# Decay selector and low-rank gate of a two-block hybrid layer: products of 48 and 16 contraction rows become products of 128 rows

## The chip, the cores and the metric

The kernel runs on one core of one Trainium2 chip. The metric is the device time of one execution in microseconds; lower is better. Three runs of the kernel before gave 1198.25, 1198.42 and 1198.77 us (median 1198.42). TensorE (PE in the rows) does the matrix products, VectorE (DVE) and ScalarE (ACT) the elementwise work, GpSimd (POOL) a few fills, and SyncE (SP) issues nearly all DMA transfers. PEld is TensorE's weight load, a separate instruction ahead of each product.

## The reference

Two model blocks run one after the other on 256 tokens of width 1024. The change lies in the first block's mixer, which has a state-space half (SSD) and a gated linear attention half (GLA). What matters of it:

```
proj = n @ w_in
z, xBC, dt_raw, q, k, v, r, a1, g_ssd, g_gla = split(proj)
# SSD: 16 heads, decay of each head
dt = softplus(dt_raw + dt_bias);  a = dt * -exp(A_log)
a_cs = cumsum(a)
Lmat = exp(a_cs[l] - a_cs[s]) where l >= s, else 0      # one matrix per head
y_diag = einsum(CB, Lmat, X)
# GLA: the gate comes from a low-rank product, 16 wide
log_alpha = log_sigmoid(a1 @ w_a2 + b_a) / 16            # a1: 256x16, w_a2: 16x512
```

`dt_raw` and `a1` are 16 columns each of `proj`; `w_a2` is a 16x512 matrix.

## The kernel before, in words

All work is laid out by a program that writes each engine's instructions in a fixed order; nothing is reordered at run time. The main stream is a series of `linear` and `tok_half` calls: products of 128x128 weight blocks with activations of 256 columns (272 in the second block), or of 128-token blocks with 512 weight columns. Both operands are split into a high and a low part in the round format fp32r, and three products (high-high, high-low, low-high; lines L403 to L405, or L454 to L456) replace one fp32 product. Such an fp32r product goes through TensorE in one pass, and a plain fp32 product is two MATMUL instructions in the trace, one behind the other.

The weights come in chunks of 8 blocks (512 KB). SP issues the load of each into one of three raw buffers (L136), ACT writes the high part (`whi`, L151), DVE subtracts to get the low part (`wlo`, L162), and so a raw buffer comes free when DVE is done with it.

Everything else is written as generators in `Side`: one step of some of them is put into the stream after every fourth weight block (`beat`, `side.tick`). PE takes what these steps issue in the middle of its stream. The products of the side work use four PSUM banks `psa` in turn (`psum_a`, so the fifth request gets the first bank again), those of the main stream four banks `psm`.

The parts that the change and the prediction speak of:

- `ev_1`, L683: the output of the block `dta1` (dt in rows 0 to 15 and 32 to 47, a1 in rows 64 to 79) is scaled into `da`, which lies in the tile `sr`, as does `wa`, the 16x512 gate matrix, loaded at L698 into rows 64 to 79. L699 and L700 load the constants and the selector.
- `rstd_0`, run in the middle of the first `linear`: the reciprocal norm, L380 and L381 on ACT, three DVE steps, then L683. PE needs L683 before it can go on, since its next output takes that bank.
- `prepare`, L574 to L577: the selector `i2` (48 rows: two unit matrices for the high and the low part of the decays), the mask `neg` and the identity are rounded to fp32r by ACT.
- `gates_gen`, L634 to L638: the running sums of the decays go to `st` (tile name `cst`), rows 0 to 15 high part, rows 32 to 47 low part.
- `decay_gen`, L646: four products for the gate, in fp32 with 16 contraction rows; ACT takes each result with L647 and L648.
- `ssd_cb`, L712 to L716: the products of B and C, a quarter into the stream of `tok_half`, which need the first `Silu` of L667 on ACT.
- `ssd_head`, L728 and L729: for j = 0, 2, 4, 6 two times two transposes (listed under L466), each pair of them into a bank of its own, and DVE scales the result into `xt`.
- `ssd_pair`, run eight times, two heads each: for each head L747 spreads that head's running sums over 128 partitions by the selector (48 contraction rows, 384 columns), L748 adds the mask to 256 of the columns; ACT takes the exponentials (L757), DVE multiplies by `cb` (L762), PE multiplies with `xt` (L768 to L772, 64 output rows for each head), DVE adds up (L776).

The two places of the change's products in the code:

```python
mm(ps, lhsT=wa[64:80, hh * P : (hh + 1) * P], rhs=da[64:80, :], start=True, stop=True)
mm(ps[:, :384], lhsT=i2[:, hd : hd + 1].to_broadcast([48, P]), rhs=st, start=True, stop=False)
```

Of the kernel before, what the change touches and what calls it, by code (L numbers as in the profile page):

```python
# [7 lines left out]
F32 = mybir.dt.float32  # L8
F32R = mybir.dt.float32r
AF = mybir.ActivationFunctionType  # L10
ALU = mybir.AluOpType
# [3 lines left out]
P = 128  # L15
D = 1024
KD = D // P
S = 256
META = 16
T = S + META  # L20
# [5 lines left out]
OFF = {}  # L26
# [204 lines left out]
def body(ctx, tc, w, lruw, vecs, cons, sels, xT, metaT, memT, wa2, gfin, out, dbg=None):  # L231
    nc = tc.nc
    act = nc.scalar.activation
    copy = nc.scalar.copy
    tt = nc.vector.tensor_tensor
    ts = nc.vector.tensor_scalar
    stt = nc.vector.scalar_tensor_tensor
    mm = nc.tensor.matmul
    side = Side()

    cp = ctx.enter_context(tc.tile_pool(name="const", bufs=1))
# [28 lines left out]
    ident = C("ident")  # L270
    eps = cp.tile([P, 1], F32, name="eps")
    nc.vector.memset(eps, EPS)
    one = cp.tile([P, 1], F32, name="one")
    nc.vector.memset(one, 1.0)
    onesD = cp.tile([P, P], F32, name="onesD")
# [17 lines left out]
    def flat(ap):  # L293
        return ap.rearrange("p a b -> p (a b)")
# [191 lines left out]
    def block1():  # L486
# [9 lines left out]
        rst = {}  # L496
# [32 lines left out]
        vG = p.tile([P, 2, D], F32, name="vG")  # L529
        sr = p.tile([P, KD, S], F32, name="sr")  # L530
        macc = p.tile([P, 2, S], F32, name="macc")
        da = sr[:80, 2, :]
        wa = flat(sr)[:80, :512]

        def ev_q(i, ps):
            e = tmp("eq")[:, :S]
# [22 lines left out]
        ssd, ssd_y = ExitStack(), ExitStack()  # L559
        sp = ssd_y.enter_context(tc.tile_pool(name="ssdy", bufs=1))  # L560
        sz = sp.tile([P, KD, S], F32, name="sz")
        st = sp.tile([48, 384], F32R, name="cst")
        i2 = sp.tile([48, 16], F32R, name="i2")
        colT = sp.tile([P, 80], F32, name="colT")
        a48 = sp.tile([P, 2, 48], F32, name="a48")
        sp = ssd.enter_context(tc.tile_pool(name="ssd", bufs=1))
# [4 lines left out]
        sel = xt.rearrange("p a b c -> p (a b c)")[:, :304]  # L571

        def prepare():
            copy(i2, sel[:48, :16])  # L574
            copy(neg, sel[:, 16:])
            copy(identR, ident)
            ts(hgn, vec[:, VEC["gla_norm"] : VEC["gla_norm"] + 2], 0.5, None, ALU.mult)  # L577
            yield
# [23 lines left out]
        def gates_gen():  # L602
            both_t = [P, 2, 16]
            U = C("trile")
            yield
            yield
            ps = psum_a()
            for t in range(2):
                transpose(ps[:, t * 16 : t * 16 + 16], da[:16, t * P : (t + 1) * P])
            v = spt[:, 7, :]  # L610
            tt(
                v.rearrange("p (t h) -> p t h", t=2), ps[:, :32].rearrange("p (t h) -> p t h", t=2),
                vec[:, VEC["dt_bias"] : VEC["dt_bias"] + 16].unsqueeze(1).to_broadcast(both_t), ALU.add,
            )
            eA = spt[:, 6, :16]
            yield
            yield from softplus_small(colT[:, :32], v, [spt[:, i, :] for i in range(6)])
            act(eA, vec[:, VEC["A_log"] : VEC["A_log"] + 16], AF.Exp)
            tabled.append(1)
            nc.gpsimd.memset(flat(a48), 0.0)  # L620
            for c in (0, 32):
                stt(
                    a48[:, :, c : c + 16], colT[:, :32].rearrange("p (t h) -> p t h", t=2), -1.0,
                    eA.unsqueeze(1).to_broadcast(both_t), ALU.mult, ALU.mult,
                )
            yield from rest(5)
            ps = psum_a()
            mm(ps[:, :32], lhsT=U, rhs=a48[:, :, :16], start=True, stop=True)
            mm(ps[:, 32:48], lhsT=one.to_broadcast([P, P]), rhs=a48[:, 0, :16], start=True, stop=True)
            for t in range(2):  # L630
                mm(ps[:48, 64 + t * P : 64 + (t + 1) * P], lhsT=a48[:, t, :], rhs=U, start=True, stop=True)
            yield
            cs = ps[:48, 64 : 64 + S]
            copy(st[:, :S], cs)  # L634
            ts(colT[:, 32:64], ps[:, :32], -1.0, None, ALU.mult)
            tt(colT[:, 64:80], ps[:, 32:48], colT[:, 32:48], ALU.add)
            tt(st[32:48, :S], cs[32:48], st[32:48, :S].bitcast(F32), ALU.subtract)
            nc.vector.tensor_copy(st[:, S:], st[:, P:S].bitcast(F32))  # L638
            show("colT", colT)

        def decay_gen():
            yield
            yield
            for hh in range(4):
                ps = psum_a()[:, :S]
                mm(ps, lhsT=wa[64:80, hh * P : (hh + 1) * P], rhs=da[64:80, :], start=True, stop=True)  # L646
                act(kt[:, hh, :], ps, AF.Identity, bias=V("gla_b_a", hh))  # L647
                act(b16[:, hh, :], ps, AF.Abs, bias=V("gla_b_a", hh))  # L648
                yield
            act(flat(b16), flat(b16), AF.Exp, scale=-1.0)  # L650
            act(flat(b16), flat(b16), AF.Ln, bias=one)
            tabled.append(1)
            yield
            msk = tmp("gm")[:, :S]
            nc.gpsimd.memset(msk, 1.0)
            nc.gpsimd.memset(msk.rearrange("p (c l) -> p c l", l=64)[:, :, 0:1], 0.0)
            for hh in range(4):
                stt(kt[:, hh, :], kt[:, hh, :], 0.0, b16[:, hh, :], ALU.min, ALU.subtract)
                nc.vector.tensor_tensor_scan(b16[:, hh, :], msk, kt[:, hh, :], 0.0, ALU.mult, ALU.add)
                yield  # L660
# [19 lines left out]
        def ev_1(i, ps):  # L680
            what, j = seq[i]
            if what == "d":
                tt(da, ps[:80], rst[0][:80], ALU.mult)  # L683
            elif what == "c":
                conv(j, ps, i < RAW)
            elif i < RAW:
                tt(sz[:, j, :], ps, rst[0], ALU.mult)
            else:
                copy(sz[:, j, :], ps)
# [5 lines left out]
        cols = [{"d": [("dta1", 0)], "z": zc, "c": xc}[a][b] for a, b in seq]  # L695
        side.add(moments())
        side.width = 1
        nc.sync.dma_start(wa[64:80, :], wa2)  # L698
        nc.sync.dma_start(con, cons)  # L699
        nc.sync.dma_start(sel, sels)  # L700
        linear(x, cols[:RAW], ev_1, S, outer=4, mid=rstd_0, at=(2, 7), spare=3)
# [32 lines left out]
                    )  # L734
                yield

        ys = Split(S)

        def ssd_pair(j):
            g = j // 4  # L740
            cps = []
# [2 lines left out]
            for i in range(2):  # L744
                hd = 2 * j + i
                ps = psum_a()
                mm(ps[:, :384], lhsT=i2[:, hd : hd + 1].to_broadcast([48, P]), rhs=st, start=True, stop=False)  # L747
                mm(ps[:, :S], lhsT=identR, rhs=neg[:, 1 : P + 1].unsqueeze(1).to_broadcast([P, 2, P]), start=False, stop=True)  # L748
                cps.append(ps)
            yield  # L750
# [2 lines left out]
            for i in range(2):  # L753
                hd = 2 * j + i
# [800 lines left out]
def matrices(i):  # L1555
    w_in = i["w_in"][0]
    dta1 = np.zeros((D, P), np.float32)
    dta1[:, :16] = dta1[:, 32:48] = w_in[:, OFF["dt"] : OFF["dt"] + 16]
    dta1[:, 64:80] = w_in[:, OFF["a1"] : OFF["a1"] + 16]
    return {  # L1560
        "w_in": w_in, "dta1": dta1, "w_up_ssd": i["w_up_ssd"][0], "w_up_gla": i["w_up_gla"][0],
        "w_o": i["w_o"][0], "w_xq": i["w_xq"][0], "w_xkv": i["w_xkv"][0], "w_xo": i["w_xo"][0],
        "w_ffn_in": i["w_ffn_in"][0], "w_ffn_out": i["w_ffn_out"][0], "w_qkv": i["sb_w_qkv_2"][0],
        "w_so": i["sb_w_o_2"][0], "w_lin": i["lru_w_in_2"][0], "w_lout": i["lru_w_out_2"][0],
        "mlp_up0": i["mlp_w_up_2"][0], "mlp_dn0": i["mlp_w_down_2"][0],
        "mlp_up1": i["mlp_w_up_2"][1], "mlp_dn1": i["mlp_w_down_2"][1],
    }
# [27 lines left out]
```

## Time and profile before

| | us |
|---|---|
| median of three runs | 1198.42 |
| the profiled execution | 1197.76 |
| its span, first to last instruction | 1195.9 |
| PE busy | 1172.1 |
| DVE busy | 813.0 |
| ACT busy | 692.7 |

The profile is of one execution, and its rows add up to that one's time: 1.86 us lie around the span, and the execution stands 0.66 us below the median of the runs. A product's duration in a row includes its way through the array, which overlaps the next product; what a product costs in a stream is the distance between its start and the next one's start.

### The profile page before, as it was taken

To read this page: it belongs to the slowest core of one execution; us is meant where nothing else is said; L and a number is where in the kernel's file an instruction comes from. 1 tells how busy PE (TensorE), PEld (TensorE's weight loads), DVE (VectorE), ACT (ScalarE), POOL (GpSimd) and SP (SyncE) were. 2 spreads that over 40 slices of the span, in tenths; PEclk is the share of its full clock that TensorE was granted. 3 is DMA by queue.
4 is the path that set the end of the run, shared out by engine and by line. 5 is a ranking of instruction groups with operands and counts; after the bars stand their busy time and mean duration, and the time that the engine had idled before them with its cause. 6 is when DMAs were issued, how large, how long until landed. Compare 5 with 4: busy or idle time off the path is not lost.

```text
span 1195.9 us, 22416 instructions
## 1 busy us (share of the span) xinstructions
PE 1172.1 (98%) x9054; PEld 1121.5 (94%) x9054; DVE 813.0 (68%) x1297; ACT 692.7 (58%) x1108; POOL 2.9 (0%) x31
## 2 busy tenths in 40 slices
PE   7999999999999999999999999999999989999997
PEld 7898899899998999999989989999999989999886
DVE  6887767877776877766676657765545887766443
ACT  6577565754655654546576656665444866665333
POOL 0000000000000000000000000000000000000000
PEclk9999999999999999999999999999999989999999
DMA  7555336375644565555623335655555535555652
GB/s 252 181 171 171 124 113 194 106 236 187 193 135 138 178 191 190 182 189 177 194 88 109 122 109 171 215 176 176 177 175 194 158 110 162 190 181 192 193 192 73
DMA packets 56855, 199.23 MB, mean 167 GB/s; under 512 B 7200, under 2 KB 8992, under 8 KB 56496
## 3 DMA queue, kind: packets, MB, share of 16 engines
q1 hardware_dynamic: 56464, 197.35, 51.9%
q8 instruction: 71, 1.16, 0.4%
q10 hardware_dynamic: 288, 0.46, 0.1%
q14 instruction: 32, 0.26, 0.1%
HBM read 196.73 MB, written 1.05 MB: 165 GB/s over the span
## 4 chain that ended last, share of the span: by engine, by line
PE 91%; DVE 3%; ACT 2%; DMA 1%; issue 1%; SPq 0%; DVEq 0%; ACTq 0%
PE psm L403 24%; PE psm L404 24%; PE psm L405 24%; PE psm L1438 2%; PE psm L1439 2%; PE psm L1440 2%; DMA wraw<-in_w_dram 1%; PE psm L454 1%; PE psm L456 1%; PE psm L455 1%; PE psa L1226 1%; ACT whi L151 1%; PE psa L747 0%; DVE iu L1391 0%; PE psa L1201 0%
## 5 line engine op out<-in xcount | busy, mean ns | idle before, releaser
L403 PE MATMUL psm<-sp_hi,whi 128*128 128x256 f32 (+1 forms) x2296 | 656.1, 286 | 7.0 <-ACT whi L151 4.6
L404 PE MATMUL psm<-sp_lo,whi 128*128 128x256 f32 (+1 forms) x2296 | 651.6, 284 | 0.5 <-DVE sp_lo L321 0.2
L405 PE MATMUL psm<-sp_hi,wlo 128*128 128x256 f32 (+1 forms) x2296 | 650.6, 283 | 0.0
L162 DVE TENSOR_TENSOR wlo<-wraw,whi 128x1024 fp32r<-128x1024 f32 (+1 forms) x339 | 412.2, 1217 | 190.1 <-ACT whi L151 186.4
L151 ACT CAST whi<-wraw 128x1024 fp32r<-128x1024 f32 (+1 forms) x339 | 353.1, 1042 | 317.9 <-PE psm L404 221.7
L403 PEld LDWEIGHTS psm<-sp_hi,whi 128*128 128x128 f32 x2296 | 433.7, 189 | 10.2 <-ACT whi L151 4.6
L404 PEld LDWEIGHTS psm<-sp_lo,whi 128*128 128x128 f32 x2296 | 433.3, 189 | 1.7 <-DVE sp_lo L321 0.9
L405 PEld LDWEIGHTS psm<-sp_hi,wlo 128*128 128x128 f32 x2296 | 433.7, 189 | 0.0
L403 PE MATMUL psm<-sp_hi,wx 128*128 128x272 f32 (+1 forms) x192 | 56.5, 294 | 3.1 <-ACT sp_hi L314 3.1
L404 PE MATMUL psm<-sp_lo,wx 128*128 128x272 f32 (+1 forms) x192 | 56.2, 293 | 0.8 <-DVE sp_lo L319 0.8
L405 PE MATMUL psm<-sp_hi,wx 128*128 128x272 f32 (+1 forms) x192 | 56.0, 291 | 0.0
L1438 PE MATMUL psm<-whi,sp_hi 128*128 128x512 f32 x128 | 50.5, 395 | 0.0
L1439 PE MATMUL psm<-wlo,sp_hi 128*128 128x512 f32 x128 | 50.4, 393 | 0.0
L1440 PE MATMUL psm<-whi,sp_lo 128*128 128x512 f32 x128 | 50.3, 393 | 0.0
L403 PEld LDWEIGHTS psm<-sp_hi,wx 128*128 128x128 f32 x192 | 37.2, 194 | 3.4 <-ACT sp_hi L314 3.3
L1499 DVE SCALAR_TENSOR_TENSOR mr<-psm,rstd 128x272 f32<-128x272 f32 (+1 forms) x64 | 27.3, 431 | 18.6 <-PE psm L405 18.4
L162 DVE TENSOR_TENSOR wx<-wraw,wx 128x1024 fp32r<-128x1024 f32 x24 | 29.4, 1223 | 14.7 <-ACT wx L151 14.7
L151 ACT CAST wx<-wraw 128x1024 fp32r<-128x1024 f32 x24 | 25.1, 1048 | 23.9 <-PE psm L404 20.5
L404 PEld LDWEIGHTS psm<-sp_lo,wx 128*128 128x128 f32 x192 | 37.1, 193 | 1.2 <-DVE sp_lo L319 1.1
L405 PEld LDWEIGHTS psm<-sp_hi,wx 128*128 128x128 f32 x192 | 37.1, 193 | 0.0
L316 ACT ACTIVATE sp_hi<-h,vec 128x256 fp32r<-128x256 f32 (+1 forms) x56 | 28.3, 510 | 6.8 <-DVE h L1408 3.4
L364 DVE TENSOR_TENSOR acc<-acc,sq 128x256 f32<-128x256 f32 (+1 forms) x63 | 26.8, 426 | 5.8 <-ACT sq L359 5.2
(384 smaller groups left out, 1226.5 us busy)
## 6 DMA issues: line engine op xcount, KB each, us to landing
wraw<-in_w_dram SPq DMA_DIRECT2D x366, 512.0 KB, 3.6
kTm<-in_memT_dram SPq DMA_DIRECT2D x1, 1024.0 KB, 5.1
gw<-in_lruw_dram SPq DMA_DIRECT2D x1, 1024.0 KB, 6.0
h<-in_xT_dram SPq DMA_DIRECT2D x3, 256.0 KB, 6.2
out_dram<-yT SPq DMA_DIRECT2D x2, 288.0 KB, 2.2
fin<-in_gfin_dram SPq DMA_DIRECT2D x1, 512.0 KB, 5.0
out_dram<-yT ACTq DMA_DIRECT2D x2, 224.0 KB, 2.6
h<-in_xT_dram SPq DMA_DIRECT2D x2, 128.0 KB, 2.5
```

The costliest lines, as they stand in the source:

```text
L151: self.nc.scalar.copy(hi[:, s], self.raw[self.done][:, s])
L162: self.nc.vector.tensor_tensor(lo[:, s], raw[:, s], hi[:, s].bitcast(F32), ALU.subtract)
L316: act(hi, src, AF.Copy, scale=scale)
L364: tt(self.acc, self.acc, sq, ALU.add)
L403: mm(ps, lhsT=wh, rhs=xh, start=start, stop=False)
L404: mm(ps, lhsT=wh, rhs=xl, start=False, stop=False)
L405: mm(ps, lhsT=wl, rhs=xh, start=False, stop=stop)
L454: mm(ps, lhsT=x.hi[:, k, s], rhs=wh, start=k == 0, stop=False)
L1438: mm(ps, lhsT=hid.hi[:, k, s], rhs=w[0], start=False, stop=False)
L1439: mm(ps, lhsT=hid.hi[:, k, s], rhs=w[1], start=False, stop=False)
L1440: mm(ps, lhsT=hid.lo[:, k, s], rhs=w[0], start=False, stop=k == kk - 1)
L1499: stt(t_, ps, 0.0, rst[0], ALU.max, ALU.mult)
```

## The change

The two kinds of small product get 128 contraction rows. For the selector, `i2` and `st` become 128 rows high; the rows that carried nothing are zero (`st` is filled with zeros by GpSimd, `i2` takes the zero rows of the selector input). For the gate, the three part products (high-high, high-low, low-high) are stacked in the rows of one fp32r product: the weights for `a1` stand three times in `dta1`, so that `da` holds a1 in rows 32, 64 and 96 onward; `wa2` is loaded three times; ACT rounds both, and DVE replaces 16 rows of each by the low part. The new tiles `wa3` and `da3` lie in the buffer `ys`, which is set up earlier for that.

```diff
+    zero = cp.tile([P, 1], F32, name="zero")
+    nc.gpsimd.memset(zero, 0.0)
...
-        da = sr[:80, 2, :]
-        wa = flat(sr)[:80, :512]
+        LOW_W, LOW_A = slice(32, 48), slice(96, 112)
+        da = sr[:, 2, :]
+        wa = flat(sr)[:, :512]
+        ys = Split(S)
+        da3 = ys.hi[:, 0, :]
+        wa3 = ys.room[0][:, 2 * T : 2 * T + 512]
...
-        st = sp.tile([48, 384], F32R, name="cst")
-        i2 = sp.tile([48, 16], F32R, name="i2")
+        st = sp.tile([P, 384], F32R, name="cst")
+        i2 = sp.tile([P, 16], F32R, name="i2")
...
         def prepare():
-            copy(i2, sel[:48, :16])
+            copy(i2, sel[:, :16])
+            nc.gpsimd.tensor_copy(st, zero.to_broadcast([P, 384]))
+            copy(wa3, wa)
+            tt(wa3[LOW_W], wa[LOW_W], wa3[LOW_W].bitcast(F32), ALU.subtract)
+            copy(da3, da)
+            tt(da3[LOW_A], da[LOW_A], da3[LOW_A].bitcast(F32), ALU.subtract)
...
-            copy(st[:, :S], cs)
+            copy(st[:48, :S], cs)
...
-            nc.vector.tensor_copy(st[:, S:], st[:, P:S].bitcast(F32))
+            nc.vector.tensor_copy(st[:48, S:], st[:48, P:S].bitcast(F32))
...
-                mm(ps, lhsT=wa[64:80, hh * P : (hh + 1) * P], rhs=da[64:80, :], start=True, stop=True)
+                mm(ps, lhsT=wa3[:, hh * P : (hh + 1) * P], rhs=da3, start=True, stop=True)
...
-                tt(da, ps[:80], rst[0][:80], ALU.mult)
+                tt(da, ps, rst[0], ALU.mult)
...
-        nc.sync.dma_start(wa[64:80, :], wa2)
+        nc.gpsimd.memset(wa, 0.0)
+        for row in (32, 64, 96):
+            nc.sync.dma_start(wa[row : row + 16, :], wa2)
...
-                mm(ps[:, :384], lhsT=i2[:, hd : hd + 1].to_broadcast([48, P]), rhs=st, start=True, stop=False)
+                mm(ps[:, :384], lhsT=i2[:, hd : hd + 1].to_broadcast([P, P]), rhs=st, start=True, stop=False)
...
-    dta1[:, :16] = dta1[:, 32:48] = w_in[:, OFF["dt"] : OFF["dt"] + 16]
-    dta1[:, 64:80] = w_in[:, OFF["a1"] : OFF["a1"] + 16]
+    dta1[:, :16] = w_in[:, OFF["dt"] : OFF["dt"] + 16]
+    for c in (32, 64, 96):
+        dta1[:, c : c + 16] = w_in[:, OFF["a1"] : OFF["a1"] + 16]
```

The order of the instructions on PE stays as it was. On ACT, at `prepare`, just behind the copies of the first half of v (L461), before:

```order
34 L461 COPY vG<-psm 128x512 x2
35 L151 CAST whi<-wraw 128x1024
36 L574 CAST i_176<-xt 48x16
37 L575 CAST neg<-xt 128x288
38 L576 CAST identR<-con 128x128
39 L590 COPY pad<-psm 128x256
```

and now, with `sr` the tile of `wa` and `da`, and `sp_hi` that of `wa3` and `da3`:

```order
34 L463 COPY vG<-psm 128x512 x2
35 L151 CAST whi<-wraw 128x1024
36 L582 CAST i_180<-xt 128x16
37 L584 CAST sp_hi<-sr 128x512
38 L586 CAST sp_hi<-sr 128x256
39 L588 CAST neg<-xt 128x288
40 L589 CAST identR<-con 128x128
41 L603 COPY pad<-psm 128x256
```

Two casts have come in ahead of the copies that empty PE's outputs. On DVE, at the same place, before:

```order
53 L162 TENSOR_TENSOR wlo<-wraw,whi 128x1024 x3
54 L577 TENSOR_SCALAR hgn<-vec 128x2
55 L162 TENSOR_TENSOR wlo<-wraw,whi 128x1024
56 L599 SCALAR_TENSOR_TENSOR xbc<-pad,vec,xbc 128x256 x3
57 L162 TENSOR_TENSOR wlo<-wraw,whi 128x1024
```

and now:

```order
53 L162 TENSOR_TENSOR wlo<-wraw,whi 128x1024 x3
54 L585 TENSOR_TENSOR sp_hi<-sr,sp_hi 16x512
55 L587 TENSOR_TENSOR sp_hi<-sr,sp_hi 16x256
56 L590 TENSOR_SCALAR hgn<-vec 128x2
57 L162 TENSOR_TENSOR wlo<-wraw,whi 128x1024
58 L612 SCALAR_TENSOR_TENSOR xbc<-pad,vec,xbc 128x256 x3
```

Two subtractions that read what those casts wrote stand ahead of the next weight chunk's low part. On SP, in the loads of the start, before:

```order
11 L136 DMA wraw<-in_w_dram 128x1024 x2
12 L698 DMA sr<-in_wa_dram 16x512
13 L699 DMA con<-in_cons_dram 128x512
14 L700 DMA xt<-in_sels_dram 128x304
15 L136 DMA wraw<-in_w_dram 128x1024 x11
```

and now:

```order
11 L136 DMA wraw<-in_w_dram 128x1024 x2
12 L713 DMA sr<-in_wa_dram 16x512 x3
13 L714 DMA con<-in_cons_dram 128x512
14 L715 DMA xt<-in_sels_dram 128x304
15 L136 DMA wraw<-in_w_dram 128x1024 x11
```

Two more issues stand ahead of the constants and of the weight chunks that follow. On POOL the fills of `zero`, `wa` and `st` are the first three instructions, ahead of all the fills that were there.

## Rows read from the trace of the kernel before

**Rows 1.** Part 1 of the page: busy us (share of the span) x instructions

```profile
PE 1172.1 (98%) x9054; PEld 1121.5 (94%) x9054; DVE 813.0 (68%) x1297; ACT 692.7 (58%) x1108; POOL 2.9 (0%) x31
```

**Rows 2.** Windows: us, then busy us of PE, PEld, DVE, ACT, POOL; clock; DMA

```profile
83.00:108.00 25.00, 25.00 (x157) 22.16 (x157) 19.82 (x35) 24.26 (x36) 0.00 (x0) 1.00 0.50 160
```

**Rows 3.** Timeline of PE, second pair: start, us, engine line op tiles xcount

```profile
114.60 0.28 PE L405 MATMUL psm<-sp_hi,wlo 128*128 128x256 f32 x1
114.81 0.44 PE L747 MATMUL psa<-cst,i 48*128 48x384 f32 x1
115.18 0.38 PE L748 MATMUL psa<-neg,identR 128*128 128x256 f32 x1
115.49 0.44 PE L747 MATMUL psa<-cst,i 48*128 48x384 f32 x1
115.86 0.39 PE L748 MATMUL psa<-neg,identR 128*128 128x256 f32 x1
116.09 0.29 PE L403 MATMUL psm<-sp_hi,whi 128*128 128x256 f32 x1
```

**Rows 4.** Timeline of PE, first gate product

```profile
74.45 0.28 PE L405 MATMUL psm<-sp_hi,sp_lo 128*128 128x256 f32 x1
74.67 0.69 PE L646 MATMUL psa<-sr 16*128 16x256 f32 x2
75.29 0.39 PE L403 MATMUL psm<-sp_hi 128*128 128x256 f32 x1
75.51 0.28 PE L404 MATMUL psm<-sp_lo,sp_hi 128*128 128x256 f32 x1
75.63 0.28 PE L405 MATMUL psm<-sp_hi,sp_lo 128*128 128x256 f32 x1
```

**Rows 5.** Timeline of PE, 512 columns, all 128 rows

```profile
100.92 0.40 PE L454 MATMUL psm<-sp_hi 128*128 128x512 f32 x1
101.16 0.39 PE L455 MATMUL psm<-sp_lo,sp_hi 128*128 128x512 f32 x1
```

**Rows 6.** Timeline of PE, second block, 432 columns, all 128 rows

```profile
633.36 0.44 PE L1226 MATMUL psa<-splo,tri 128*128 128x432 f32 x1
633.64 0.23 PE L1227 MATMUL psa<-splo,ones 128*128 128x144 f32 x1
```

**Rows 7.** Timeline of PE, behind products of 64 output rows

```profile
161.85 0.39 PE L403 MATMUL psm<-sp_hi,whi 128*128 128x256 f32 x1
162.08 0.28 PE L404 MATMUL psm<-sp_lo,whi 128*128 128x256 f32 x1
```

**Rows 8.** Line L314, its form of 512 columns (ACT)

```profile
L314 ACT CAST sp_hi<-sz x4: 618/620/624, 177.0 to 184.5; 128x512 fp32r<-128x512 f32 x4
```

**Rows 9.** Line L637 (DVE)

```profile
L637 DVE TENSOR_TENSOR cst<-psa,cst x1: 418/418/418, 74.7 to 74.7; 16x256 fp32r<-16x256 f32 x1
```

**Rows 10.** Timeline of ACT, at the last gate product [idle before <-releaser]

```profile
82.12 0.48 ACT L647 ACTIVATE kt<-psa,vec 128x256 f32<-128x256 f32 x1 [1.01 <-PE psa L646]
```

**Rows 11.** Timeline of DVE, results of the first transposes

```profile
106.33 0.75 DVE L729 TENSOR_TENSOR xt<-psa,colT 128x256 f32<-128x256 f32 x2
```

**Rows 12.** Timeline of PE, third group of transposes

```profile
109.58 0.60 PE L466 MATMUL psa<-con,xbc 128*128 128x128 f32 x4
```

**Rows 13.** Waits of ACT between 50 and 180: us in total, times, longest

```profile
ACT E L757 <- PE psa L748: 7.7, 5, 2.8
```

**Rows 14.** Timeline of SP, loads of the start

```profile
13.72 0.43 SPq L700 DMA_DIRECT2D xt<-in_sels_dram  x1
```

**Rows 15.** Line L136 (SP), the load issued at 23.6

```profile
L136 SPq DMA_DIRECT2D wraw<-in_w_dram x1: 328/328/328, 23.6 to 23.6; - x1
...
DMA to landing us min/median/max: 4.1/4.1/4.1
```

**Rows 16.** Timeline of ACT, before the reciprocal norm

```profile
27.86 1.05 ACT L151 CAST whi<-wraw 128x1024 fp32r<-128x1024 f32 x1 [1.37 <-PE psa L375]
```

**Rows 17.** Timeline of PE, after the reciprocal norm

```profile
32.02 0.36 PE L403 MATMUL psm<-sp_hi,whi 128*128 128x256 f32 x1 [1.04 <-DVE sr L683]
```

More of the change, by code (lines that the diff above doesn't have):

```diff
@@ L735, in ssd_head @@
                 yield
-        ys = Split(S)
         def ssd_pair(j):
```

## The prediction, made before the changed kernel ran

> **What bounds the kernel now.** I read the page's engine line first, then busy time by windows around the change, then PE's timeline at the two small products, last the waits. The engine line shows PE busy 98% of the span [rows 1]; what shortens PE's own stream shortens the kernel, unless something else is then late. The windows say where that could be: from 83 to 108 us PE has no idle time, and ACT is busy 24.26 of 25 us [rows 2]. There the two run side by side, PE with no lead to speak of.
>
> In PE's timeline I read distances between starts. In the stream two passes of 256 columns stand 0.12 apart (75.51 to 75.63) [rows 4]. One pair of heads costs more than its columns: from L405 at 114.60 to L403 at 116.09 are 1.49 us, for five steps (L405, L747, L748, L747, L748): 0.21, 0.37, 0.31, 0.37, 0.23 [rows 3]. L748 has 256 columns and 128 rows like L403, and still takes 0.31 ahead of an L747. What differs is that the contraction rows change from 128 to 48 and back, four times. The gate product shows the same: from L405 at 74.45 to L404 at 75.51 are 1.06 us, with two passes of L646 (16 rows, fp32) between [rows 4].
>
> **The change part by part.** *Gate products.* The stacked product is one fp32r pass of 128 rows and 256 columns, like its neighbours. From L405 to the second product behind it are then three steps of 0.12, 0.36 in place of 1.06: 0.70 less, four times: **2.8 us**.
>
> *Selector products.* With 128 rows everywhere L748 should step on after 0.12. L747 has 384 columns; no row shows that at 128 rows. Rows of 512 columns step by 0.24 [rows 5], so the middle to 0.12 is 0.18. The other end is L1226: 432 columns, 128 rows, 0.28 to the next product [rows 6], where short products with weights of their own follow. L748 is not short, so I take 0.18 and keep 0.28 for the range. A pair is then 0.12 + 0.18 + 0.12 + 0.18 + 0.12 = 0.72; against 1.49 that is 0.77 less. By their order three of the eight pairs stand right behind L772, which has 64 output rows. That change of shape stays: behind such products the first full one steps by 0.23 (161.85 to 162.08) [rows 7], not 0.12. For those three I leave the entry as it is and give the first L747 0.23: from L747 to L403 0.23 + 0.12 + 0.18 + 0.12 = 0.65 in place of 1.28 (114.81 to 116.09) [rows 3], 0.63 less. Sum: 5 x 0.77 + 3 x 0.63 = **5.7 us**; with all eight alike 6.2.
>
> *Work added in `prepare`.* ACT gets a cast of 512 columns, 0.62 [rows 8], and one of 256, between half of that and all of it: about 0.9 together. DVE gets two subtractions, 0.42 for 256 columns [rows 9] and between one and two times that for 512, say 0.7: 1.1 together. Behind them are queued the next chunk's low part and the copies of PE's outputs, so I let the side work run 1.1 late from there. At 82.12 that meets a wait of ACT, 1.01 for the fourth gate product [rows 10], which comes 2.8 earlier now. So the ACT chain of 83 to 108 us starts 1.1 - 1.0 = 0.1 late, and not early.
>
> *What is late next.* By then PE has gained 2.8 from the gate and 0.77 from the first pair, 3.6 in all, and ACT and DVE nothing. They meet at the transposes. The third group (j = 4) takes the banks that DVE empties with the first two L729; these end at 106.33 + 0.75 = 107.08 [rows 11], PE's four transposes start at 109.58 and the second bank is taken about 0.2 later, at 109.8 [rows 12]. Moved up by 3.6 PE would be there at 106.2, with the bank free at 107.08 + 0.1 = 107.2: **1.0 us of wait**. It is nothing if ACT and DVE come along earlier, and 2.0 if their full 1.1 arrives. Behind that ACT waits for PE at five of the pairs [rows 13], so the remaining gain of seven pairs should stand.
>
> *The start.* SP issues two more loads at 0.43 each [rows 14], so the weight loads behind them can move by 0.9. Does it matter? The reciprocal norm on ACT is queued behind the cast at 27.86. The profile puts that cast's wait to PE's L375, but its load, issued at 23.6, takes 4.1 to land, which is 27.8 [rows 15, 16]. And PE waits 1.04 us for what follows from it (L683, at 32.02) [rows 17]. Loads are issued as raw buffers come free, so a late load makes a later one late, and what arrives there adds to PE's wait in full. Between 0 (the memory queue is full then, and takes the delay) and 0.9 I take **0.4 us**. The zero fills on POOL lie ahead of everything; POOL is busy 2.9 us in the whole span [rows 1], so I cost them at nothing. If SP's first `wa` load had to wait for them, it would add to the 0.4. The rows that `da` gained cost nothing: L637 takes 0.42 for 16 rows [rows 9], so rows are not what a DVE instruction's time goes by.
>
> *Sum.* 2.8 + 5.7 - 1.0 - 0.4 = 7.1. The profiled execution took 1197.76, so 1190.7 by its own time; it lies 0.66 below the median of 1198.42, so the forecast is **1191.3 us**. Ends: with all pairs alike, no wait and no late start 2.8 + 6.2 = 9.0 less, 1189.4; with sixteen L747 at 0.28 (1.6), a wait of 2.0 and a start of 0.9 it is 8.5 - 1.6 - 2.0 - 0.9 = 4.0 less, 1194.4.
>
> **The rivals.** *Rows do not count.* Then L747 keeps its 0.37, and of the gate only one of two passes goes, 0.3 each (74.67 to 75.29 are two), 1.2 in all; less 0.4 at the start: 0.8 less, 1197.6. For it: the sum of work is the same number of columns. Against it: L748, untouched and of full height, costs 0.31 next to L747 and L403 0.12 next to its like [rows 3, 4].
> The Trainium skill speaks for this rival in "TensorE: Matmul & The Clock Gate": "LDWEIGHTS (loading the stationary operand)" says that loading weights goes by columns and not by contraction rows, and the table in "Why this matters for your kernels" that one product of 32 rows takes the time of one of 128. By that the result would be this rival's. The skill's "TensorEngine Tiling (Array Packing)", "Key Properties", says the contrary for a mixed stream: "Changing tiling mode (not just tile) drains the TensorE". The rows just named decide for the second.
>
> *The side work becomes the bound (slower).* If ACT and DVE pace PE not only at the transposes but through all pairs, PE waits out whatever it gains, and the side work's 1.1 and the start's 0.4 come on top: 1198.42 + 1.5 = 1199.9. It decides from the point where the 7.7 us that ACT now waits for PE's L748 [rows 13] are used up. The pairs give back 5.7, so that is near but not reached. For it: ACT's 24.26 of 25 us [rows 2]. Against it: behind 108 ACT has those waits at all, so PE leads there and not ACT.
>
> *Only the gate gains.* If the pair's steps are set by something else that L747 and L748 share (both go into the same bank, with the other's weights loaded between), 2.8 remain, less 0.4, and nothing is lost at the transposes: with a lead of 2.8 PE is there at 107.0, 0.2 of wait. That is 2.2 less, 1196.2. Against it: L403 to L405 also share a bank and change weights, at 0.12.
>
> **How the numbers follow.** Forecast 0.78, rows do not count 0.08, side work 0.09, only the gate 0.05. A change under 0.2% (2.4 us, so from 1196.0 to 1200.8) is about what cannot be told from none. Faster is the forecast's 0.78 and most of the last, together 0.82; slower is the upper part of the side-work case, whose 1199.9 with 0.9 at the start and more delay passes 1200.8: 0.04; the same is the rest, 0.14. The range of 8 in 10 is the likeliest case's own, 1189.4 to 1194.4, opened to 1189.0 and, toward the other cases, to 1196.0.
>
> **What would show it.** Right: the gate product with four MATMULs in place of eight and steps of 0.12 on both sides; L747's steps near 0.18 and L748's at 0.12; a new PE wait near 1 us at the transposes, put to DVE's `xt`; PE's wait behind the reciprocal norm near 1.4 in place of 1.04. Wrong: L747 still at 0.37, or PE idle at several pairs and ACT no longer waiting for L748.

## The result and the profile after

The changed kernel took 1191.87 us (median of four runs, 1190.36 to 1192.93) beside 1198.60 us for the kernel before on the same chip: a ratio of 0.9946, 95% interval 0.9934 to 0.9958, 6.7 us less. Run again later, together with the kernel before and three of the experiments below, it took 1190.91 us against 1198.53, ratio 0.9934, interval 0.9920 to 0.9947. The forecast was 1191.3 us, with a range of 1189.0 to 1196.0. The profiled execution took 1190.99 us, with a span of 1188.9 in place of 1195.9; its rows explain those 7.0 us.

Line numbers have moved: the stream's products L403 to L405 are now L405 to L407, the gate product is L659 (L646 before), the selector product L760 (L747), the mask's product L761 (L748), the transposes L468 (L466), DVE's scaling behind them L744 (L729).

Part 1 of the page, busy us and instructions of each engine, answers to [rows 1]:

```profile
PE 1163.6 (98%) x9050; PEld 1119.4 (94%) x9050; DVE 813.0 (68%) x1299; ACT 693.1 (58%) x1110; POOL 3.9 (0%) x34
```

PE has four products fewer, one for each gate product; DVE and ACT have the two subtractions and two casts more. PE is still the engine that bounds.

PE's timeline at the first gate product (start, us, engine line, op, operands, tiles, count), answers to [rows 4]:

```profile
74.87 0.28 PE L407 MATMUL psm<-sp_hi,sp_lo 128*128 128x256 f32 x1
74.99 0.28 PE L659 MATMUL psa<-sp_hi 128*128 128x256 f32 x1
75.11 0.28 PE L405 MATMUL psm<-sp_hi 128*128 128x256 f32 x1
75.23 0.28 PE L406 MATMUL psm<-sp_lo,sp_hi 128*128 128x256 f32 x1
```

From L407 to L406 are 0.36 us, where 1.06 were: the gate product now steps like any other of its stream. The second pair of heads, PE's timeline, answers to [rows 3]:

```profile
112.36 0.28 PE L407 MATMUL psm<-sp_hi,wlo 128*128 128x256 f32 x1
112.47 0.33 PE L760 MATMUL psa<-cst,i 128*128 128x384 f32 x1
112.64 0.28 PE L761 MATMUL psa<-neg,identR 128*128 128x256 f32 x1
112.76 0.34 PE L760 MATMUL psa<-cst,i 128*128 128x384 f32 x1
112.94 0.28 PE L761 MATMUL psa<-neg,identR 128*128 128x256 f32 x1
113.05 0.28 PE L405 MATMUL psm<-sp_hi,whi 128*128 128x256 f32 x1
```

The five steps take 0.69 us in place of 1.49. L761, which the change did not touch, now steps by 0.12 where it took 0.31. Behind products of 64 output rows the first selector product is slower, 0.28 (120.62 to 120.90):

```profile
120.30 0.39 PE L785 MATMUL psa<-E,xt 128*64 128x128 f32 x4
120.62 0.44 PE L760 MATMUL psa<-cst,i 128*128 128x384 f32 x1
120.90 0.28 PE L761 MATMUL psa<-neg,identR 128*128 128x256 f32 x1
121.02 0.34 PE L760 MATMUL psa<-cst,i 128*128 128x384 f32 x1
121.19 0.28 PE L761 MATMUL psa<-neg,identR 128*128 128x256 f32 x1
```

What was given back on the way: PE's waits between 20 and 170 us (total, times, longest), in the kernel after:

```profile
PE psm L405 <- DVE sr L696: 1.2, 1, 1.2
PE psa L468 <- DVE xt L744: 0.6, 1, 0.6
PE psa L377 <- DVE acc L366: 0.5, 1, 0.5
```

The first is the wait behind the reciprocal norm, 1.04 before [rows 17]. The third stands at 27.24 us, ahead of the norm, where the profile of before has none. The second is new and stands at the third transposes; DVE's L744, which empties their banks, has moved from 106.33 [rows 11] to 106.72, while PE has come forward. DVE's and then PE's timeline there, the latter answering to [rows 12]:

```profile
106.72 0.75 DVE L744 TENSOR_TENSOR xt<-psa,colT 128x256 f32<-128x256 f32 x2
```

```profile
106.28 0.28 PE L407 MATMUL psm<-sp_hi,wlo 128*128 128x256 f32 x1
107.19 0.77 PE L468 MATMUL psa<-con,xbc 128*128 128x128 f32 x4 [0.63 <-DVE xt L744]
107.71 0.36 PE L405 MATMUL psm<-sp_hi,whi 128*128 128x256 f32 x1
```

The four transposes take 0.77 where they took 0.60: the second bank comes 0.17 late too. From L407 to L405 are 1.43 us; without a wait they are 0.48 (106.50 to 106.98 in a run shown below), so 0.95 is lost.

Setting the start of the same product in both timelines side by side gives the account of the profiled execution (minus is earlier than before):

| where | us |
|---|---|
| behind the reciprocal norm, 32.02 to 32.31, and 0.13 more by 70 us | +0.4 |
| four gate products | -2.8 |
| first pair | -0.8 |
| third transposes: the wait, and 0.2 more at the second bank | +1.0 |
| the seven other pairs | -4.9 |
| all that follows, 160 us to the end | 0.0 |
| sum | -7.1 |

### The profile page after: what moved, and what is told of

It reads as the page before. It is cut to its first block, busy times and chain, and to the rows that moved or that the text cites. A ratio compares the mean times of both kernels' runs of the same rounds, so it can differ in the third digit from the quotient of the medians.

```text
span 1188.9 us, 22416 instructions
## 1 busy us (share of the span) xinstructions
PE 1163.6 (98%) x9050; PEld 1119.4 (94%) x9050; DVE 813.0 (68%) x1299; ACT 693.1 (58%) x1110; POOL 3.9 (0%) x34
## 3 DMA queue, kind: packets, MB, share of 16 engines
q8 instruction: 71, 1.16, 0.4%
## 4 chain that ended last, share of the span: by engine, by line
PE 85%; ACT 5%; DVE 5%; DMA 3%; issue 2%; SPq 0%; ACTq 0%; DVEq 0%
PE psm L405 23%; PE psm L406 23%; PE psm L407 23%; DMA wraw<-in_w_dram 3%; PE psm L1451 2%; PE psm L1452 2%; PE psm L1453 2%; ACT whi L151 2%; DVE wlo L162 1%; PE psa L1239 1%; PE psm L456 1%; PE psm L457 1%; PE psm L458 1%; PE psa L1214 0%; PE psa L377 0%
## 5 line engine op out<-in xcount | busy, mean ns | idle before, releaser
L405 PE MATMUL psm<-sp_hi,whi 128*128 128x256 f32 (+1 forms) x2296 | 655.7, 286 | 6.8 <-ACT whi L151 4.7
L406 PE MATMUL psm<-sp_lo,whi 128*128 128x256 f32 (+1 forms) x2296 | 651.3, 284 | 0.9 <-DVE sp_lo L323 0.9
L407 PE MATMUL psm<-sp_hi,wlo 128*128 128x256 f32 (+1 forms) x2296 | 650.4, 283 | 0.0
L162 DVE TENSOR_TENSOR wlo<-wraw,whi 128x1024 fp32r<-128x1024 f32 (+1 forms) x339 | 412.0, 1216 | 189.8 <-ACT whi L151 187.1
L151 ACT CAST whi<-wraw 128x1024 fp32r<-128x1024 f32 (+1 forms) x339 | 353.1, 1042 | 318.8 <-PE psm L406 199.5
L405 PEld LDWEIGHTS psm<-sp_hi,whi 128*128 128x128 f32 x2296 | 433.5, 189 | 9.7 <-ACT whi L151 4.7
L406 PEld LDWEIGHTS psm<-sp_lo,whi 128*128 128x128 f32 x2296 | 433.1, 189 | 1.8 <-DVE sp_lo L323 1.3
L407 PEld LDWEIGHTS psm<-sp_hi,wlo 128*128 128x128 f32 x2296 | 433.5, 189 | 0.0
L405 PE MATMUL psm<-sp_hi,wx 128*128 128x272 f32 (+1 forms) x192 | 56.7, 295 | 3.1 <-ACT sp_hi L316 3.1
L406 PE MATMUL psm<-sp_lo,wx 128*128 128x272 f32 (+1 forms) x192 | 56.3, 293 | 0.8 <-DVE sp_lo L321 0.8
L407 PE MATMUL psm<-sp_hi,wx 128*128 128x272 f32 (+1 forms) x192 | 56.1, 292 | 0.0
L405 PEld LDWEIGHTS psm<-sp_hi,wx 128*128 128x128 f32 x192 | 37.2, 194 | 3.4 <-ACT sp_hi L316 3.3
L162 DVE TENSOR_TENSOR wx<-wraw,wx 128x1024 fp32r<-128x1024 f32 x24 | 29.4, 1223 | 14.6 <-ACT wx L151 14.6
L151 ACT CAST wx<-wraw 128x1024 fp32r<-128x1024 f32 x24 | 25.1, 1048 | 24.1 <-PE psm L406 21.0
L406 PEld LDWEIGHTS psm<-sp_lo,wx 128*128 128x128 f32 x192 | 37.2, 194 | 1.2 <-DVE sp_lo L321 1.1
L407 PEld LDWEIGHTS psm<-sp_hi,wx 128*128 128x128 f32 x192 | 37.2, 194 | 0.0
```

What stands on the lines that cost most here:

```text
L151: self.nc.scalar.copy(hi[:, s], self.raw[self.done][:, s])
L162: self.nc.vector.tensor_tensor(lo[:, s], raw[:, s], hi[:, s].bitcast(F32), ALU.subtract)
L405: mm(ps, lhsT=wh, rhs=xh, start=start, stop=False)
L406: mm(ps, lhsT=wh, rhs=xl, start=False, stop=False)
L407: mm(ps, lhsT=wl, rhs=xh, start=False, stop=stop)
```

## The experiments

Each ran on one chip together with the kernel before and with the others of its group: the selector alone, the gate alone, the padded gate and both parts moved (before: 1198.28); the fewer changes of rows, the casts early, the loads late and the changed kernel again (1198.53); the selector at 96 and at 64 rows (1198.33). Repeated runs of one kernel spread by 0.7 to 2.7 us, so half a microsecond between two medians is not told apart here; the steps in the timelines are.

**The selector alone.** The kernel before with `st` and `i2` of 128 rows, the gate as it was.

```diff
-        st = sp.tile([48, 384], F32R, name="cst")
+        st = sp.tile([P, 384], F32R, name="cst")
...
-                mm(ps[:, :384], lhsT=i2[:, hd : hd + 1].to_broadcast([48, P]), rhs=st, start=True, stop=False)
+                mm(ps[:, :384], lhsT=i2[:, hd : hd + 1].to_broadcast([P, P]), rhs=st, start=True, stop=False)
```

> Only the selector product of the change, 128 rows with zeros; the gate product as before. Theory of the forecast: 5.7 us by the forecast's terms, 5.3 to 5.6 by the steps measured behind the change (entry of three pairs 0.28 and not 0.23), no wait at the transposes, since PE comes there with 0.8 us of lead only, and no later start: ratio 0.9953 to 0.9956. If the sum of this and of the gate alone passes the whole change (6.7 us) by more than 1 us, the two meet at a wait; the theory says by about 0.6 to 1.0. Rival (rows do not count): 0.

Measured: 1192.73 us, 5.6 less, ratio 0.9954 (0.9941 to 0.9968). From the first pair to the end of the last, PE's starts move forward by 5.6 us against the profile of before. There is no wait at the transposes.

**The gate alone.** The change with the selector back at 48 rows.

```diff
-        st = sp.tile([P, 384], F32R, name="cst")
+        st = sp.tile([48, 384], F32R, name="cst")
...
-                mm(ps[:, :384], lhsT=i2[:, hd : hd + 1].to_broadcast([P, P]), rhs=st, start=True, stop=False)
+                mm(ps[:, :384], lhsT=i2[:, hd : hd + 1].to_broadcast([48, P]), rhs=st, start=True, stop=False)
```

> The stacked gate product of the change with its casts, subtractions and three loads; the selector products stay at 48 rows. Theory of the forecast (a change of contraction rows costs PE, each stacked product gives back 0.70 us): 4 x 0.70 = 2.8 us, less 0.3 at the start (two more SP issues), and a wait at the third transposes of 0 to 0.2, since PE gets there with a lead of 2.8 and not 3.6: 2.3 to 2.5 us under the kernel before, ratio 0.998. Rival (rows do not count, only passes): four passes fewer at 0.3, 1.2 less 0.3 = 0.9 under. Rival (the added side work paces PE): 0 to 1.5 us slower.

Measured: 1196.31 us, 2.0 less, ratio 0.9983 (0.9975 to 0.9992), under the 2.3 to 2.5 expected and over the rival's 0.9. The timeline shows the four products give back 2.8 us here as well; but PE came 1.2 us later than before from the reciprocal norm in this profile (below). The two parts alone sum to 7.5 us; the whole gave 6.7 and 7.6, so the 0.6 to 1.0 us that were to be lost where they meet can't be read from the medians.

**Rows or passes.** The selector at 128 rows, and the gate as an fp32 product of two passes, the 16 rows of `wa` padded with zeros to 128: no stacking, no casts, no more loads.

```diff
-        da = sr[:80, 2, :]
-        wa = flat(sr)[:80, :512]
+        da = sr[:, 2, :]
+        wa = flat(sr)[:, :512]
...
-                mm(ps, lhsT=wa[64:80, hh * P : (hh + 1) * P], rhs=da[64:80, :], start=True, stop=True)
+                mm(ps, lhsT=wa[:, hh * P : (hh + 1) * P], rhs=da, start=True, stop=True)
...
+        nc.gpsimd.memset(wa, 0.0)
```

> The selector products with 128 rows as in the change; the gate's product stays an fp32 product of two passes, but with 128 rows, of which 112 are zeros, so without casts, subtractions or more loads. Theory of the forecast (the change of rows is what costs): selector 5.3 to 5.6, and of each gate product the excess over its passes: two fp32 passes at 0.12 to 0.3 and steps of 0.12 on both sides, 1.06 to 0.7 or less, 4 x 0.3 to 0.4 = 1.2 to 1.6; less a wait at the transposes of 0 to 0.6: 6.2 to 7 us under the kernel before, so within 0.5 us of the whole change. Rival (in the gate the passes cost and not the rows): as the selector alone, 5.3 to 5.6 under.

Measured: 1190.50 us, 7.8 less, ratio 0.9937 (0.9924 to 0.9949), over the 6.2 to 7 expected; in its profile PE's starts have moved by 6.9 when the pairs are done. PE's timeline at the first gate product (L649):

```profile
74.75 0.28 PE L407 MATMUL psm<-sp_hi,sp_lo 128*128 128x256 f32 x1
74.86 0.60 PE L649 MATMUL psa<-sr 128*128 128x256 f32 x2
75.11 0.47 PE L405 MATMUL psm<-sp_hi 128*128 128x256 f32 x1
75.42 0.28 PE L406 MATMUL psm<-sp_lo,sp_hi 128*128 128x256 f32 x1
```

From L407 to L406 are 0.67 us. Of the gate's 0.70, then, 0.39 (1.06 to 0.67) come from the rows alone and 0.31 (0.67 to 0.36) from one fp32r pass in place of two fp32 passes. That is more than one step of 0.12, and no run here divides it further. This kernel is as fast as the change: it gains 0.3 x 4 less at the gate and has neither the casts' delay nor the wait at the transposes.

**Fewer changes of rows.** The kernel before, with 48 rows, but the two L747 of a pair one behind the other and then its two mask products.

```diff
                 mm(ps[:, :384], lhsT=i2[:, hd : hd + 1].to_broadcast([48, P]), rhs=st, start=True, stop=False)
-                mm(ps[:, :S], lhsT=identR, rhs=neg[:, 1 : P + 1].unsqueeze(1).to_broadcast([P, 2, P]), start=False, stop=True)
                 cps.append(ps)
+            for ps in cps:
+                mm(ps[:, :S], lhsT=identR, rhs=neg[:, 1 : P + 1].unsqueeze(1).to_broadcast([P, 2, P]), start=False, stop=True)
```

> The kernel before, with 48 rows, but each pair's two selector products one behind the other and then the two products of 256 columns: the same four products, two changes of contraction rows in place of four. Theory (each change of rows costs PE): per pair the excess of 0.77 falls by about half, 0.3 to 0.4, over eight pairs 2.4 to 3.2 us under the kernel before, ratio 0.9973 to 0.998; the second selector product, behind its like, shows a step near 0.18 to 0.25, the second of the others 0.12. Rival (48 rows make each product slow in itself, whatever stands beside it): 0, with the steps of 0.37 unchanged. Rival (the weights or the bank that change between the four): 0 or slower, since every product here still has weights and a bank other than its neighbour's.

Measured: 1194.59 us, 3.9 less, ratio 0.9969 (0.9957 to 0.9980), over the 2.4 to 3.2 expected. The second pair in PE's timeline:

```profile
114.33 0.28 PE L405 MATMUL psm<-sp_hi,wlo 128*128 128x256 f32 x1
114.54 0.61 PE L747 MATMUL psa<-cst,i 48*128 48x384 f32 x2
115.07 0.51 PE L750 MATMUL psa<-neg,identR 128*128 128x256 f32 x2
115.42 0.28 PE L403 MATMUL psm<-sp_hi,whi 128*128 128x256 f32 x1
```

The same four products take 1.09 us with two changes of rows, 1.49 with four [rows 3], 0.69 with none: 0.20 for each change, and 0.39 for the gate's two. Over the eight pairs PE's starts move by 3.1 us in the profile, which is what was expected; the rest of the 3.9 does not show in the pairs. The five steps are 0.21, 0.28, 0.26, 0.23 and 0.12: about half of each change falls on the step ahead of it, half on the first product behind it. Two changes cost half of what four cost, with the same two products of 48 rows, so nothing is left for these products in themselves. Nor for the banks, which now change at every step, or for the weight loads, still one for each product.

**How many rows are another height.** The changed kernel with the selector at 96 and at 64 rows (the edit for 96; 64 alike).

```diff
-        st = sp.tile([P, 384], F32R, name="cst")
+        st = sp.tile([96, 384], F32R, name="cst")
...
-                mm(ps[:, :384], lhsT=i2[:, hd : hd + 1].to_broadcast([P, P]), rhs=st, start=True, stop=False)
+                mm(ps[:, :384], lhsT=i2[:, hd : hd + 1].to_broadcast([96, P]), rhs=st, start=True, stop=False)
```

> The changed kernel with the selector's product over 96 rows in place of 128 (48 of them zeros): asks which heights count as another one. Theory A (any number of rows other than the neighbours' 128 costs as 48 did): steps of 0.21, 0.37, 0.31, 0.37, 0.22 in a pair again, about 5.3 us over the changed kernel, near 1196.3, the time of the stacked gate alone. Theory B (96 rows use as much of the array's height as 128): steps of 0.12, 0.18, 0.12, 0.18, 0.12, no difference from the changed kernel, 1190.9 to 1191.9. Theory C (the cost goes by the rows that are missing): 32 of 80 missing rows, 0.4 x 5.3 = 2.1 us over, near 1193.3.

> The same with 64 rows (16 of them zeros). Theory A and theory B: as 48 rows, steps of 0.21, 0.37, 0.31, 0.37, 0.22, about 5.3 us over the changed kernel, near 1196.3. Theory C: 64 of 80 missing rows, 0.8 x 5.3 = 4.2 us over, near 1195.5. If 64 rows step like 128, the bound lies between 48 and 64.

Measured: 1191.18 us with 96 rows, ratio 0.9942 (0.9925 to 0.9958); 1196.72 with 64, ratio 0.9985 (0.9976 to 0.9994). PE's timeline, second pair, with 96 rows:

```profile
112.16 0.28 PE L407 MATMUL psm<-sp_hi,wlo 128*128 128x256 f32 x1
112.28 0.34 PE L760 MATMUL psa<-cst,i 96*128 96x384 f32 x1
112.46 0.28 PE L761 MATMUL psa<-neg,identR 128*128 128x256 f32 x1
112.58 0.34 PE L760 MATMUL psa<-cst,i 96*128 96x384 f32 x1
```

and with 64:

```profile
112.38 0.28 PE L407 MATMUL psm<-sp_hi,wlo 128*128 128x256 f32 x1
112.59 0.44 PE L760 MATMUL psa<-cst,i 64*128 64x384 f32 x1
112.95 0.38 PE L761 MATMUL psa<-neg,identR 128*128 128x256 f32 x1
113.27 0.44 PE L760 MATMUL psa<-cst,i 64*128 64x384 f32 x1
113.64 0.39 PE L761 MATMUL psa<-neg,identR 128*128 128x256 f32 x1
113.86 0.29 PE L405 MATMUL psm<-sp_hi,whi 128*128 128x256 f32 x1
```

This is theory B: 96 rows step like 128 (0.18 and 0.12), 64 rows like 48 (0.36 and 0.32). What counts is not the number of rows but on which side of a bound between 64 and 96 it lies; a cost that goes by the missing rows (theory C) would have given 1193.3 and 1195.5.

**The wait at the transposes and the start.** Three variants of the changed kernel: both moved, only the casts and subtractions queued early, only the three loads issued late; and the changed kernel itself once more.

```diff
             side.add(normed_x())
+            side.add(stacked())
+
+        def stacked():
+            LOW_W, LOW_A = slice(32, 48), slice(96, 112)
+            copy(wa3, wa)
+            copy(da3, da)
+            yield
+            tt(wa3[LOW_W], wa[LOW_W], wa3[LOW_W].bitcast(F32), ALU.subtract)
+            tt(da3[LOW_A], da[LOW_A], da3[LOW_A].bitcast(F32), ALU.subtract)
...
-            copy(wa3, wa)
-            tt(wa3[LOW_W], wa[LOW_W], wa3[LOW_W].bitcast(F32), ALU.subtract)
-            copy(da3, da)
-            tt(da3[LOW_A], da[LOW_A], da3[LOW_A].bitcast(F32), ALU.subtract)
```

```diff
         def rstd_0():
             side.finish()
             rst[0] = mom.rstd()
+            for row in (32, 64, 96):
+                nc.sync.dma_start(wa[row : row + 16, :], wa2)
...
-        for row in (32, 64, 96):
-            nc.sync.dma_start(wa[row : row + 16, :], wa2)
```

> The whole change, but the three loads of the gate's weights are issued behind the first weight loads and not ahead of them, and the two casts and two subtractions are queued early, in the idle time that ACT and DVE have before the norm's products, and not behind it. Theory of the forecast: the later start (0.3) and the wait at the third transposes (0.6) are gone, and PE's wait behind the reciprocal norm is near 1.04 again: 0.8 to 1.2 us under the changed kernel, about 1190.9 beside its 1191.87. Rival (the end of the side work of 83 to 108 us bounds anyway): the casts are only moved, ACT's chain stays where it was and the wait stays at 0.6: 0.3 under the changed kernel. Rival: the subtractions hold up the low parts of the input on DVE and the start gets later: slower than the changed kernel.

> The changed kernel once more, unedited, as the yardstick on the same chip for the two runs that move its prepared work. Measured so far: 1191.87 us, with runs from 1190.36 to 1192.93. Expected from every theory: 1191 to 1192.5, a wait of 0.6 us at the third transposes.

> The changed kernel with its two casts and two subtractions queued early (in idle time of ACT and DVE, before the products of the norm's result), the three loads where the change has them. Theory of the forecast (the wait at the third transposes comes from the side work that the casts made late): the wait of 0.6 is gone, the small delays of PE near 67 to 70 us (0.1 to 0.4) too: 0.6 to 0.9 us under the changed kernel. Rival (the loads and the start made the difference of the version with both): as the changed kernel, within 0.3.

> The changed kernel with only its three small loads issued behind the first weight loads, the casts where the change has them. Theory of the forecast (two more issues on SP make the start 0.4 later): 0.3 to 0.4 us under the changed kernel, with PE's wait behind the reciprocal norm at 1.04 or less, and the wait at the third transposes larger by the same, 0.6 to 0.9, so that 0 to 0.4 remain. Rival (the start differs from one execution to the next by when TensorE's clock falls and rises, and the two issues cost nothing): no difference beyond 0.5 either way, and a start that spreads in the profiles whatever the loads do.

Measured: both moved 1190.33 us (1189.53 to 1190.63), the casts alone 1190.43 (1190.07 to 1191.21), the loads alone 1190.21 (1189.42 to 1190.63), the changed kernel again 1190.91 (1189.58 to 1191.57). All three lie under both medians of the changed kernel, by 0.5 to 1.7, but their ranges overlap with its own: a version that beats it is not shown.

In the timelines the wait at the transposes is plain: what counts is how DVE's emptying of the banks stands to PE's arrival. PE and DVE with the casts early (there the scaling is L748):

```profile
106.50 0.28 PE L407 MATMUL psm<-sp_hi,wlo 128*128 128x256 f32 x1
106.62 0.60 PE L468 MATMUL psa<-con,xbc 128*128 128x128 f32 x4
106.98 0.36 PE L405 MATMUL psm<-sp_hi,whi 128*128 128x256 f32 x1
```

```profile
104.63 0.75 DVE L748 TENSOR_TENSOR xt<-psa,colT 128x256 f32<-128x256 f32 x2
```

There is no wait: DVE is 1.2 us ahead. PE in the changed kernel's second profile, where DVE's L744 begins at 106.78:

```profile
107.00 0.28 PE L407 MATMUL psm<-sp_hi,wlo 128*128 128x256 f32 x1
107.25 0.77 PE L468 MATMUL psa<-con,xbc 128*128 128x128 f32 x4
107.77 0.36 PE L405 MATMUL psm<-sp_hi,whi 128*128 128x256 f32 x1
```

From L407 to L405 are 0.77, so 0.3 is lost and not 0.95: DVE stands where it stood in the first profile (106.72), but PE comes 0.7 later. With the loads late 0.3 is lost too, and not the 0.6 to 0.9 expected. How much of the wait the casts make is less plain. The scaling begins between 106.18 and 107.17 in the six profiles that have the casts in `prepare` (mean 106.62), between 105.70 and 106.43 in the four without casts (106.08), and at 104.63 and 106.26 in the two with the casts early; in the second of these, both moved, 0.2 is still lost. The means give the casts 0.5; the spread within each group is larger.

The traces show what the scaling follows. ACT's L151 for one weight load waits until that load has landed. Before:

```profile
75.95 1.05 ACT L151 CAST whi<-wraw 128x1024 fp32r<-128x1024 f32 x1 [1.40 <-DMA wraw<-in_w_dram]
```

and in the first and the second profile of the changed kernel:

```profile
77.48 1.05 ACT L151 CAST whi<-wraw 128x1024 fp32r<-128x1024 f32 x1 [1.51 <-DMA wraw<-in_w_dram]
77.54 1.05 ACT L151 CAST whi<-wraw 128x1024 fp32r<-128x1024 f32 x1 [0.67 <-DMA wraw<-in_w_dram]
```

In the nine profiles in which ACT has no wait left for a gate product, the scaling begins 29.2 to 29.6 us behind this cast, 29.24 in both of the changed kernel. SP issues the load when DVE has freed its raw buffer: DVE's subtraction L162 ends at 71.8 before and at 73.26 after, and the load goes out at 71.82 and 73.29. Counted from the first product behind the norm the load goes out after 39.0 to 39.8 us in the six profiles without the casts at that place and 40.9 to 41.2 in the six with them: the casts and subtractions make the load later, and that is shown. But the same load took 3.3 to 5.1 us to land, 4.2 in the first profile of the changed kernel and 3.5 in the second. So how much of the delay reaches the banks differs from one execution to the next.

Why PE comes late to that place in the second profile shows at the start. PE's busy time and granted clock there, second profile and then first (columns: window, length, busy, clock, DMA share, GB/s):

```profile
12.00:14.00 2.00, 1.14 (x6) 0.53 0.70 259
14.00:16.00 2.00, 2.00 (x11) 0.50 0.77 250
16.00:18.00 2.00, 2.00 (x12) 0.50 0.95 303
```

```profile
12.00:14.00 2.00, 1.25 (x10) 1.00 0.74 237
14.00:16.00 2.00, 2.00 (x19) 1.00 0.91 280
16.00:18.00 2.00, 2.00 (x19) 1.00 1.01 345
```

The same kernel ran these 6 us at 1.2 GHz in one execution and at 2.4 in the other. PE had been busy for 0.33 us of the two before (10 to 12) in the one, 0.98 in the other. With the lower clock the first product behind the reciprocal norm stands at 33.07 and not at 32.31. Against the 32.02 of before it stands, in the other profiles, at +0.65 (casts early), +1.16 (gate alone), +0.49 and +0.60 (96 and 64 rows), all with the three loads ahead; at +0.50 and +0.75 with the loads late; at -0.53, +0.15 and +0.30 without the added loads. Moving the loads late does not bring the start forward as expected: with the loads alone moved they are issued at 31.06, behind the cast at 28.35 that the norm follows, so that profile's +0.50 is not theirs. Sorted by the clock: in the four profiles at 2.4 GHz from 12 us to the norm the product stands at 32.31 with the loads ahead, and at 31.49, 32.02 and 32.52 without them there. In the eight with a stretch at 1.2 GHz it stands at 32.51 to 33.18 (mean 32.81) with them ahead and at 32.17, 32.32 and 32.77 (mean 32.42) without. So 0.3 to 0.4 goes with the loads and 0.4 to 0.5 with the clock, but the groups are small and overlap: that the loads cost it is not shown.

## Why the prediction was right

- *Gate, 2.8 us.* Right: 0.36 in place of 1.06 each, and 2.8 in the account. The pad experiment splits it into 0.39 of rows and 0.31 of the one fp32r pass for two fp32 passes. "Rows do not count" would have left the 0.39 and is refuted by it.
- *Selector, 5.7 us.* Right: 0.8 + 4.9 in the account. L760 steps by 0.17 to 0.18, the middle that was taken, and L761 by 0.12; only the first L760 of the first pair takes 0.26 (96.37 to 96.63). Two small errors cancel: the four other pairs in the plain stream give 0.80 (1.49 to 0.69) and not 0.77, and the three behind products of 64 output rows keep 0.28 for the first selector product and not 0.23, 0.15 too much in all.
- *Work added in `prepare`, 0.9 on ACT and 1.1 on DVE.* 1.02 (0.614 and 0.401) and 1.10 (0.681 and 0.421), and the load named above is issued 1.2 later against the norm. ACT's wait of 1.01 for the fourth gate product is gone, as forecast. DVE's L744 stands 0.4 later (106.33 to 106.72), of which 0.3 is the later start, so against the norm it is the 0.1 of the forecast. In the second profile it is 0.6 earlier against the norm, since the load landed 0.7 sooner. The forecast had no term for the landing, and that 0.1 came out in the first profile is partly luck.
- *The wait at the third transposes, 1.0.* Right place and size in the first profile, 0.95, and DVE's banks are what PE waits for; 0.3 in the second, where PE was late itself and DVE was not. The added work is part of the cause, as the issue of the load shows; the size is that of one execution.
- *The start, 0.4.* The profile shows 0.3 at that product, and sorting by the clock gives the loads 0.3 to 0.4 in the mean, but the reason given is not shown. The start moved from -0.5 to +1.2 us among executions with and without the loads, and TensorE's clock took part in it. That the term fitted the first profile is partly luck.
- *The rivals.* Rows do not count: refuted by the padded gate and by the order of 48-row products. The Trainium skill's "TensorE: Matmul & The Clock Gate", "Why this matters for your kernels", gives one product of 32 rows the time of one of 128. The run with two changes of rows in place of four agrees for products of 48 rows taken by themselves; the 0.20 us for each change come on top in a mixed stream. The Trainium skill's "TensorEngine Tiling (Array Packing)", "Key Properties", says that changing the tiling mode drains TensorE. The 64-row run agrees, and 0.20 us is this case's price. Side work as the bound: ACT waited 7.7 us for PE at the pairs [rows 13], and still waits 3.1 for L761, so the seven pairs stood. Only the gate gains: refuted by the selector alone.

## What to carry to other kernels

In a stream of full-height products, count the changes of contraction height rather than the rows: each cost 0.20 us here, more than a product of 256 columns (0.12), and zeros in the unused rows removed it at no price in the stream. Where the operands can't be padded, products of one height one behind the other share the change (3.1 us of 5.6). Read such costs as distances between starts, and look at the neighbours: the untouched full-height product carried 0.2 us of the cost.

## What the runs showed of the hardware

- A product of 96 contraction rows stepped with its neighbours of 128 like one of their own, one of 64 rows did not (0.18 against 0.36).
- Behind products of 64 output rows, too, the first product of full size paid: 0.28 in place of 0.17 for 384 columns, with 0.20 between the last of them and it (120.42 to 120.62). They keep that price in the changed kernel. If each entry and exit of the eight groups costs the 0.20 of a change of height, it is 3.2 us in all; that is an estimate, and no run here took it away.
- The granted clock between 12 and 18 us was 1.00 in one execution of the changed kernel and 0.50 to 0.53 in another. Of the 0.8 us that PE came later from the norm, 0.7 went where the wait at the transposes shrank from 0.95 to 0.3; behind the pairs the two stand 0.1 apart.
- The spans of the two are 0.6 us apart (1188.9 and 1189.5), and 0.5 of it arises near 981 us, in the second block, which the change does not touch. Behind a wait of PE for ACT (3.07 us in both) the granted clock is 0.50 from 978 to 980 us in both, and from 980 to 982 us 0.95 in the one and 0.63 in the other.
